# One order for VectorE's weight steps from SwiGLU on, other rooms for the last product, and outputs copied out of PSUM before they are finished

## The chip, the cores and the metric

The kernel runs on one core of one Trainium2 chip. The core has a matrix engine (TensorE, PE in the profile, with PEld for its weight loads), a vector engine (VectorE, DVE), a scalar engine (ScalarE, ACT), GpSimd (POOL), and a queue engine (SyncE, SP) that issues almost all DMA transfers. The metric is the device time of one execution in microseconds (us); lower is better.

## The reference

One layer of a decoder trunk runs on 256 tokens of width 2048, in float32. The part that the change touches is the feed-forward end of the layer:

```python
def swiglu(h, w_ffn_in, w_ffn_out):
    gate, up = jnp.split(h @ w_ffn_in, 2, axis=-1)
    return (jax.nn.silu(gate) * up) @ w_ffn_out

        h = rms_norm(x, norm2_gain[l]) * (1 + scale2) + shift2
        x = x + gate2 * swiglu(h, w_ffn_in[l], w_ffn_out[l])
```

`w_ffn_in` is 2048 x 11264 and `w_ffn_out` 5632 x 2048. Before it come conditioning (`mod`), a first norm, the input projection, three token mixers (stick-breaking attention, dilated attention, gated linear attention) and their output projection.

## The kernel before

**Arithmetic.** A float32 product is made of three matmuls on a reduced float32 format (`mm3`, lines 170 to 172): activation-high by weight-high, activation-high by weight-low, activation-low by weight-high. Each weight tile of 128 x 1024 (two 128-row chunks of 512 columns, 512 KB) is loaded once and "halved": ScalarE casts it to its high half (L166), and VectorE subtracts that from the raw tile to get the low half (L167). The halves live in `whi` and `wlo`, four rooms each, in rotation (`halves_room`).

**Rooms for raw tiles.** `raw_tile` (L149 on, issue on L159) hands out rooms in rotation: four in the `raw` pool, and then those in `rooms["extra"]`. The counter runs on over the whole kernel and is taken modulo the number of rooms. The DMA is issued on SP, which works in order: a load whose room is still in use holds up the loads behind it on that queue.

**Paired blocks.** From the second SwiGLU block on, and in the last product, two column blocks b0 and b1 are worked together for the first few row groups (`paired`, L1217 on). A group is four 128-row chunks, in two halves (`c` = 0 and 2). Its four raw tiles are r0 = (c 0, b0), r1 = (c 0, b1), r2 = (c 2, b0), r3 = (c 2, b1). From them VectorE forms four differences (`differ`, L1230): t1 = r1 - r0, t2 = r3 - t1, t3 = r3 - r1 and t4 = r2 - t2. t1 and t3 go to the first of a group's two `places`, t2 and t4 to the second. Then r0, t1, t2, r2 and t3 are halved in this order (`first`) and feed five products (`product`), six matmuls each and group. After that a loop (`rest`) takes two more row chunks of b0 (a plain halved weight) and one more halved tile (r3 of each group, then t4 of each group) per round, 18 matmuls a round. In SwiGLU there is one group (n = 1); in the last product two (n = 2). Sums of products go from a PSUM bank through `held` (ScalarE) and are added into two other banks by VectorE (L1252).

**SwiGLU.** Eleven blocks (`for i in range(NFF)`). In block i the gate columns come first and then the up columns; from i = 1 the two are paired, and the up columns go on with twelve more row chunks (L1315, six halved tiles). From the end of i = 0 the raw rooms are the pool's four and A4 and A8. The activations are h2, whose high halves lie in H0 to H3 and low halves in H4 to H7, four row chunks each; left-hand sums of h2 lie in A2 and A3. The places of the group are A13 and A14. VectorE also works on `gate2` meanwhile: steps on L287, each placed behind the last halving that had been traced (`mac`).

**The last product.** `w_fo` is `w_ffn_out`. Column blocks 0 and 1 are a pair, then 2 and 3. For n = 0 (and again n = 2) the raw rooms are the pool's four and H4 to H7; the two groups' places are A13, A14 and H2, H3. After the pair the b1 column block goes on alone over the remaining 36 row chunks. For n = 3 the last 14 row chunks are loaded as seven halved tiles, of which three have their halves in H2 to H7 (`spare`), and the two token tiles follow each other. `add_out` multiplies a PSUM bank by `gate2` (L1343), adds the residual x2 (L1345) and stores it (L1347). x2 is read back from DRAM into A2, A3, A4 and A8 (L1331).

**Order.** The framework orders the instructions of each engine by priority and by when its own model of the run has them ready, and it sets all semaphores. `prio()` raises the priority of what is inside by 4000 steps. `tc.issue_after(x)` places what it encloses behind x on x's engine and adds no semaphore.

Of the kernel before, what the change touches and what calls it, by code (L numbers as in the profile page):

```python
# [10 lines left out]
F32 = mybir.dt.float32  # L11
# [3 lines left out]
ALU = mybir.AluOpType  # L15
AX = mybir.AxisListType

P = 128
T = 256
NT = T // P  # L20
# [47 lines left out]
def trunk(ctx: ExitStack, tc: tile.TileContext, I, out):  # L68
# [16 lines left out]
    def S(tag, shape, dtype=F32):  # L85
        return slot.tile(shape, dtype, tag=tag, name=nm(tag))
# [64 lines left out]
    def raw_tile(src, ka, b, n=2):  # L151

        i = rooms["n"] % (4 + len(rooms["extra"]))
        rooms["n"] += 1
        if i < 4:
            raw = wp.tile([P, 2, NB], F32, tag="raw", name=nm("raw"))
        else:
            raw = S(rooms["extra"][i - 4], [P, 2, NB])
        nc.sync.dma_start(raw[:, :n, :], src[b][:, ka : ka + n, :])  # L159
        return raw  # L160
# [3 lines left out]

    def halve(hi, lo, raw):
        nc.scalar.copy(hi, raw)  # L166
        state["split"] = nc.vector.tensor_tensor(lo, raw, hi.bitcast(F32), op=ALU.subtract)  # L167

    def mm3(ps, lh, ll, rh, rl, start, stop, seeded=False):
        nc.tensor.matmul(ps, lh, rh, start=start, stop=False, skip_group_check=seeded)  # L170
# [1046 lines left out]
    def paired(act, sums, places, src, b0, b1, p0, p1, k1):  # L1217

        (c11, c21), (c12, c22) = p0, p1
        n = len(sums)  # L1220
        side, held = misc_bank([P, NB]), scr([P, NB])

        def halved(raw):
            hi, lo = halves_room()
            halve(hi, lo, raw)
            return hi, lo

        def differ(x, y, tag=None, into=None):
            d = S(tag, [P, 2, NB]) if into is None else into
            nc.vector.tensor_tensor(d, x, y, op=ALU.subtract)  # L1230
            return d

        with prio():
            raws = [(raw_tile(src, 4 * g, b0), raw_tile(src, 4 * g, b1)) for g in range(n)]
            raws = [r + (raw_tile(src, 4 * g + 2, b0), raw_tile(src, 4 * g + 2, b1)) for g, r in enumerate(raws)]
            first = [halved(r[0]) for r in raws]
            t1 = [differ(r[1], r[0], p[0]) for p, r in zip(places, raws)]
            first += [halved(t) for t in t1]
            t2 = [differ(r[3], t, p[1]) for p, r, t in zip(places, raws, t1)]
            first += [halved(t) for t in t2]  # L1240
            first += [halved(r[2]) for r in raws]
            first += [halved(differ(r[3], r[1], p[0])) for p, r in zip(places, raws)]
        rest = []
        for q in range(2 * n):
            g, k = q % n, 4 * n + 2 * q
            w = load_weights(src, k, k + 2, b0)
            with prio():
                rest.append((w, halved(raws[g][3] if q < n else differ(raws[g][2], t2[g], into=t2[g]))))

        def add(dst):  # L1250
            with prio(2 * AHEAD):
                nc.vector.tensor_tensor(dst, c21, held, op=ALU.add)  # L1252

        def times(ps, left, right, g, start=False):
            hi, lo = right
            for i in range(2):
                h, l = left(g, i)
                mm3(ps, h, l, hi[:, i, :], lo[:, i, :], start and i == 0, i == 1, seeded=True)

        def product(ps, left, start=False):  # L1260
            for g in range(n):
                times(ps, left, first.pop(0), g, start and g == 0)

        total = lambda q: lambda g, i: (sums[g][0][:, q, i, :], sums[g][1][:, q, i, :])
        part = lambda c, t: lambda g, i: act(4 * g + c + i, t)
        product(c11, part(0, 0), True)
        with prio(2 * AHEAD):
            nc.scalar.copy(c21, c11)
        product(side, total(0), True)
        with prio(2 * AHEAD):  # L1270
            nc.scalar.copy(held, side)
        product(c21, total(1))
        add(c12)
        product(c11, part(2, 0))
        product(c21, total(2))
        add(c22)
        for q, (w, right) in enumerate(rest):
            k = 4 * n + 2 * q
            block(p0, act, None, k, k + 2, 0, w=w, go_on=True, more=True, seeded=True)
            if q < n:  # L1280
                times(c12, total(3), right, q)
            else:
                times(c21, part(2, 1), right, q - n)
        block(p0, act, src, 8 * n, k1, b0, go_on=True, seeded=True)

    for i in range(NFF):
        pg = [acc_bank() for _ in range(NT)]
        if i == 0:
            w = load_weights(w_ff, 0, KC, 0, spare=("A12", "KD", "A9", "A10", "A0", "A1", "T1", "T2"))
            for t in range(NT):  # L1290
                block(pg, h2_at, None, 0, KC, 0, w=w, tiles=(t,))
            bg.append(gate2_bg())
            pu = [acc_bank() for _ in range(NT)]
        else:
            pu = [acc_bank() for _ in range(NT)]
            state["rate"] = (2 if i < 7 else 4) * RATE_FFN
            paired(h2_at, h2_sums, [("A13", "A14")], w_ff, i, NFF + i, pg, pu, KC)
            state["rate"] = 0.0
            if i in LATE:
                assert not macs  # L1300
                with prio():
                    act_sums.append(left_sums(LATE[i], ("A13", "A14"), *act[i - min(LATE)]))
        sgs = []
        with prio():
            for t in range(NT):
                sg = scr([P, NB])
                nc.scalar.activation(sg, pg[t], AF.Silu)
                sgs.append(sg)
        if i == 0:
            block(pu, h2_at, w_ff, 0, KC, NFF)  # L1310
            h2_sums = [left_sums(("A2", "A3"), ("A13", "A14"), h2[0][0], h2[1][0])]
            rooms["extra"] = ("A4", "A8")
        else:
            block(pu, h2_at, w_ff, 4, KC, NFF + i, go_on=True, seeded=True)
        hi = S(ftags[2 * i], [P, 4, T], F32R)  # L1315
        lo = S(ftags[2 * i + 1], [P, 4, T], F32R)
        with prio():
            for t in range(NT):
                nc.vector.tensor_mul(sgs[t], sgs[t], pu[t])

        def turn(sgs=sgs, hi=hi, lo=lo):
            for t in range(NT):
                transpose_split(sgs[t], hi, lo, t)

        later.append(turn)
        act.append((hi, lo))
    rooms["extra"] = ()
    x2 = []
    for n in range(4):
        xr = S(("A2", "A3", "A4", "A8")[n], [P, NT, NB])  # L1330
        nc.sync.dma_start(xr, x2_far[:, n])  # L1331
        x2.append(xr)

# [18 lines left out]
    K0 = 4 * len(act_sums)  # L1352
    for n in range(4):
        if n % 2 == 0:
            rooms["extra"] = ("H4", "H5", "H6", "H7")
            both = [[acc_bank() for _ in range(NT)] for _ in range(2)]
            paired(act_at, act_sums, [("A13", "A14"), ("H2", "H3")], w_fo, n, n + 1, *both, KF)
        pss = both[n % 2]
        if n == 3:
            rooms["extra"] = ()  # L1360
            block(pss, act_at, w_fo, K0, CUT, n, more=True, go_on=True, seeded=True)
            w = load_weights(w_fo, CUT, KF, n, spare=[f"H{j}" for j in range(2, 8)])
            block(pss, act_at, None, CUT, KF, 0, w=w, tiles=(0,), go_on=True, seeded=True)
            with prio():
                add_out(n, 0, pss[0])

            block(pss, act_at, None, CUT, KF - LASTK, 0, w=w, tiles=(1,), go_on=True, more=True, seeded=True)
            side = acc_bank()
            for cols, ps in ((slice(0, NB - LASTC), pss[1][:, : NB - LASTC]), (slice(NB - LASTC, NB), side[:, :LASTC])):
                for k in range(KF - LASTK, KF):  # L1370
                    wh, wl = w[k - CUT]
                    h, l = act_at(k, 1)
                    mm3(ps, h, l, wh[:, cols], wl[:, cols], k == KF - LASTK and cols.start > 0, k == KF - 1, seeded=True)
                if cols.start == 0:
                    add_out(n, 1, pss[1], end=NB - LASTC)
                    add_out(n, 1, pss[1], NB - LASTC, store=False)
            add_out(n, 1, side, NB - LASTC, base=NB - LASTC)
        else:
            if n == 1:
                block(pss, act_at, w_fo, K0, KF, n, go_on=True, seeded=True)  # L1380
            if n == 0:
                flush()
                gate2 = state["gate2"]
            with prio():
                for t in range(NT):
                    add_out(n, t, pss[t])


_INS = ["x", "c", "b_ada", "norm1_gain", "norm2_gain", "sb_q_gain", "sb_k_gain", "dil_q_gain", "dil_k_gain", "w_gla_a",
# [44 lines left out]
```

## Time and profile before

| what | value |
|---|---|
| median of three runs | 1627.28 us (1623.92, 1627.28, 1629.01) |
| the profiled execution | 1626.09 us |
| its span, first to last instruction | 1624.3 us |
| TensorE busy | 1592.4 us, 98% |
| VectorE busy | 1242.4 us, 76% |
| ScalarE busy | 855.2 us, 53% |
| DMA engines, mean busy over the span | 74% |

The page of the profile gives busy time by engine, the span in 40 slices, the chain of work that ended last, groups of instructions by line, and DMA issues. Matmuls overlap each other, so that a matmul of 0.39 us starts every 0.23 us; the start-to-start distance is what counts. Times within the run are microseconds from the start of the span. SwiGLU's second block begins near 1030 us, the last product near 1369 us, and the second pair of the last product near 1498 us.

### The profile page before, as it was taken

The numbers are of one execution on the slowest core, as the hardware profiler recorded it, in microseconds if no ns is written. First come the engines' busy times: TensorE is split into PE (matmuls) and PEld (weight loads), VectorE is DVE, ScalarE is ACT, GpSimd is POOL, SyncE is SP. The second block draws the span as 40 slices with busy tenths as digits, with TensorE's granted clock in tenths as the row PEclk, the third lists the DMA queues.
The fourth block names the chain that finished last, engine by engine and source line by source line (L and its number), as shares of the span: only waits on it lengthen the run. The fifth ranks groups of instructions, "written<-read, shape, count | busy, mean of one in ns | idle before, by whom it ended". The sixth has DMA issues, their size and how long they took to land.

```text
span 1624.3 us, 20044 instructions
## 1 busy us (share of the span) xinstructions
PE 1592.4 (98%) x7269; PEld 1311.2 (81%) x7269; DVE 1242.4 (76%) x1418; ACT 855.2 (53%) x1180; POOL 5.4 (0%) x14
## 2 busy tenths in 40 slices
PE   8999999999999999999999999999999998999999
PEld 7878888788777888888887888888888886788787
DVE  6889995877779787878657788888888875755754
ACT  5654449756587444444445555555555553534432
POOL 1000000000000000000000000000000000000000
PEclk9999999999999999999999999999999999999999
DMA  8999997874767888888776577777776666665653
GB/s 325 354 326 323 325 312 224 281 267 136 249 231 233 265 305 311 314 289 314 236 219 226 161 252 253 259 254 252 245 232 194 185 190 224 206 200 178 211 154 114
DMA packets 116179, 399.24 MB, mean 246 GB/s; under 512 B 13090, under 2 KB 13896, under 8 KB 116080
## 3 DMA queue, kind: packets, MB, share of 16 engines
q1 hardware_dynamic: 115856, 397.95, 74.0%
q8 instruction: 57, 0.93, 0.2%
q14 instruction: 42, 0.34, 0.1%
q0 software_dynamic: 224, 0.01, 0.0%
HBM read 393.71 MB, written 4.19 MB: 245 GB/s over the span
## 4 chain that ended last, share of the span: by engine, by line
PE 89%; DVE 4%; DMA 3%; ACT 2%; issue 1%; POOL 0%; DVEq 0%; ACTq 0%; POOLq 0%
PE acc L172 27%; PE acc L171 27%; PE acc L170 27%; DVE wlo L167 2%; ACT whi L166 1%; PE misc L1071 1%; DMA H<-w_ffn_out 1%; PE acc L430 1%; DMA AR<-ada_rest 1%; PE misc L786 1%; DMA raw<-w_ffn_out 1%; PE misc L170 1%; PE misc L171 1%; PE misc L172 1%; DMA raw<-w_in 0%
## 5 line engine op out<-in xcount | busy, mean ns | idle before, releaser
L166 ACT CAST whi<-raw 128x1024 fp32r<-128x1024 f32 (+1 forms) x449 | 459.4, 1028 | 483.1 <-PE acc L172 365.0
L167 DVE TENSOR_TENSOR wlo<-raw,whi 128x1024 fp32r<-128x1024 f32 (+1 forms) x449 | 531.1, 1191 | 223.0 <-ACT whi L166 219.2
L170 PE MATMUL acc<-whi,H 128*128 128x512 f32 x1476 | 578.7, 392 | 0.8 <-ACT H L442 0.4
L171 PE MATMUL acc<-wlo,H 128*128 128x512 f32 x1476 | 578.0, 392 | 1.1 <-DVE wlo L167 1.0
L172 PE MATMUL acc<-whi,H 128*128 128x512 f32 x1476 | 578.1, 392 | 1.0 <-DVE H L1157 0.6
L172 PEld LDWEIGHTS acc<-whi,H 128*128 128x128 f32 x1476 | 278.1, 189 | 59.8 <-DVE H L449 1.8
L170 PEld LDWEIGHTS acc<-whi,H 128*128 128x128 f32 x1476 | 278.1, 188 | 58.3 <-ACT H L442 1.3
L171 PEld LDWEIGHTS acc<-wlo,H 128*128 128x128 f32 x1476 | 278.1, 188 | 58.0 <-DVE wlo L167 2.2
L166 ACT CAST whi<-A 128x1024 fp32r<-128x1024 f32 x98 | 103.0, 1054 | 89.1 <-PE acc L172 85.5
L167 DVE TENSOR_TENSOR wlo<-A,whi 128x1024 fp32r<-128x1024 f32 x98 | 118.7, 1221 | 30.8 <-ACT whi L166 29.9
L170 PE MATMUL acc<-whi,A 128*128 128x512 f32 x332 | 130.5, 393 | 6.7 <-ACT whi L166 6.7
L171 PE MATMUL acc<-wlo,A 128*128 128x512 f32 x332 | 129.8, 391 | 0.0
L172 PE MATMUL acc<-whi,A 128*128 128x512 f32 x312 | 122.0, 391 | 0.0
L287 DVE SCALAR_TENSOR_TENSOR ada<-AR,csil,ada 128x1024 f32<-128x1024 f32 x59 | 75.1, 1279 | 6.8 <-DMA AR<-ada_rest 6.8
L170 PEld LDWEIGHTS acc<-whi,A 128*128 128x128 f32 x332 | 62.6, 188 | 20.6 <-ACT whi L166 7.7
L166 ACT CAST whi<-H 128x1024 fp32r<-128x1024 f32 x41 | 43.0, 1053 | 63.7 <-PE acc L172 40.4
L167 DVE TENSOR_TENSOR wlo<-H,whi 128x1024 fp32r<-128x1024 f32 x41 | 49.9, 1223 | 34.2 <-ACT whi L166 29.2
L171 PEld LDWEIGHTS acc<-wlo,A 128*128 128x128 f32 x332 | 62.6, 188 | 13.4 <-DVE wlo L167 0.4
L172 PEld LDWEIGHTS acc<-whi,A 128*128 128x128 f32 x312 | 58.8, 189 | 12.1
L170 PE MATMUL acc<-whi,T 128*128 128x512 f32 x120 | 46.8, 390 | 0.0
L172 PE MATMUL acc<-whi,T 128*128 128x512 f32 x120 | 46.7, 389 | 0.0
L171 PE MATMUL acc<-wlo,T 128*128 128x512 f32 x120 | 46.7, 389 | 0.0
(402 smaller groups left out, 1556.7 us busy)
## 6 DMA issues: line engine op xcount, KB each, us to landing
raw<-w_in SPq DMA_DIRECT2D x203, 512.0 KB, 4.9
raw<-w_ffn_in SPq DMA_DIRECT2D x122, 512.0 KB, 4.5
AR<-ada_rest SPq DMA_DIRECT2D x79, 512.0 KB, 4.8
A<-w_ffn_in SPq DMA_DIRECT2D x54, 512.0 KB, 4.4
raw<-w_ffn_out SPq DMA_DIRECT2D x53, 512.0 KB, 4.3
H<-w_ffn_out SPq DMA_DIRECT2D x35, 512.0 KB, 4.5
raw<-w_out SPq DMA_DIRECT2D x32, 512.0 KB, 4.5
KC<-ada_rest SPq DMA_DIRECT2D x30, 512.0 KB, 5.3
```

What stands on the lines that cost most here:

```text
L166: nc.scalar.copy(hi, raw)
L167: state["split"] = nc.vector.tensor_tensor(lo, raw, hi.bitcast(F32), op=ALU.subtract)
L170: nc.tensor.matmul(ps, lh, rh, start=start, stop=False, skip_group_check=seeded)
L171: nc.tensor.matmul(ps, lh, rl, start=False, stop=False, skip_group_check=seeded)
L172: state["mm"] = nc.tensor.matmul(ps, ll, rh, start=False, stop=stop, skip_group_check=seeded)
L287: nc.vector.scalar_tensor_tensor(acc, raw, c, acc, op0=ALU.mult, op1=ALU.add)
L430: state["warm"] = nc.tensor.matmul(ps, ones_r, wide, start=True, stop=True)
L786: nc.tensor.matmul(ps[:n, t * N_GLA + h, :].rearrange("p (s l) -> p s l", l=L), at(f, h, t)[:, :n], odd(at(f, h, t)), start=True, stop=True,)
L1071: nc.tensor.transpose(ps[:, i, :], src[:, i * P : (i + 1) * P], ident)
```

## The change

`halve`'s subtraction and `differ` now go through one helper, `in_order`. Once `state["ordered"]` is set, at the end of SwiGLU's first block, each of them is placed on VectorE behind the one that was traced before it. `paired` traces the differences t1 and t2 of all groups ahead of the first halving, t3 behind t1's halving, and t4 at the front of the first rounds of `rest` instead of in its last rounds. The raw tiles are loaded in the order r0, r1, r3, r2, each for all groups. In the last product the raw rooms beside the pool's four are A4 and A8 for the first pair, and A4, A8, H2 and H3 for the second; the second group's places are A2 and A3; x2 is read into H4 to H7. For n = 1 and n = 2 ScalarE first copies the two PSUM banks to a tile in H4, and `add_out` then works from there without raised priority.

```diff
     def halve(hi, lo, raw):
         nc.scalar.copy(hi, raw)
-        state["split"] = nc.vector.tensor_tensor(lo, raw, hi.bitcast(F32), op=ALU.subtract)
+        state["split"] = in_order(lo, raw, hi.bitcast(F32), op=ALU.subtract)
+
+    def in_order(*args, **kw):
+
+        with tc.issue_after(state["split"].ins) if "ordered" in state else nullcontext():
+            return nc.vector.tensor_tensor(*args, **kw)
...
         def differ(x, y, tag=None, into=None):
             d = S(tag, [P, 2, NB]) if into is None else into
-            nc.vector.tensor_tensor(d, x, y, op=ALU.subtract)
+            state["split"] = in_order(d, x, y, op=ALU.subtract)
             return d
 
         with prio():
-            raws = [(raw_tile(src, 4 * g, b0), raw_tile(src, 4 * g, b1)) for g in range(n)]
-            raws = [r + (raw_tile(src, 4 * g + 2, b0), raw_tile(src, 4 * g + 2, b1)) for g, r in enumerate(raws)]
-            first = [halved(r[0]) for r in raws]
+            raws = {(c, b, g): raw_tile(src, 4 * g + c, b) for c, b in ((0, b0), (0, b1), (2, b1), (2, b0)) for g in range(n)}
+            raws = [[raws[c, b, g] for c in (0, 2) for b in (b0, b1)] for g in range(n)]
             t1 = [differ(r[1], r[0], p[0]) for p, r in zip(places, raws)]
-            first += [halved(t) for t in t1]
             t2 = [differ(r[3], t, p[1]) for p, r, t in zip(places, raws, t1)]
-            first += [halved(t) for t in t2]
-            first += [halved(r[2]) for r in raws]
-            first += [halved(differ(r[3], r[1], p[0])) for p, r in zip(places, raws)]
+            first = [halved(r[0]) for r in raws] + [halved(t) for t in t1]
+            t3 = [differ(r[3], r[1], p[0]) for p, r in zip(places, raws)]
+            first += [halved(t) for t in t2] + [halved(r[2]) for r in raws] + [halved(t) for t in t3]
         rest = []
         for q in range(2 * n):
             g, k = q % n, 4 * n + 2 * q
+            if q < n:
+                with prio():
+                    differ(raws[g][2], t2[g], into=t2[g])
             w = load_weights(src, k, k + 2, b0)
             with prio():
-                rest.append((w, halved(raws[g][3] if q < n else differ(raws[g][2], t2[g], into=t2[g]))))
+                rest.append((w, halved(raws[g][3] if q < n else t2[g])))
...
             rooms["extra"] = ("A4", "A8")
+            state["ordered"] = True
...
-    rooms["extra"] = ()
     x2 = []
     for n in range(4):
-        xr = S(("A2", "A3", "A4", "A8")[n], [P, NT, NB])
+        xr = S(f"H{4 + n}", [P, NT, NB])
         nc.sync.dma_start(xr, x2_far[:, n])
...
         if n % 2 == 0:
-            rooms["extra"] = ("H4", "H5", "H6", "H7")
+            rooms["extra"] = ("A4", "A8", "H2", "H3")[: 2 + n]
             both = [[acc_bank() for _ in range(NT)] for _ in range(2)]
-            paired(act_at, act_sums, [("A13", "A14"), ("H2", "H3")], w_fo, n, n + 1, *both, KF)
+            paired(act_at, act_sums, [("A13", "A14"), ("A2", "A3")], w_fo, n, n + 1, *both, KF)
...
-            w = load_weights(w_fo, CUT, KF, n, spare=[f"H{j}" for j in range(2, 8)])
+            w = load_weights(w_fo, CUT, KF, n, spare=("H2", "H3", "H4", "H5", "A2", "A3"))
...
                 gate2 = state["gate2"]
+                with prio():
+                    for t in range(NT):
+                        add_out(n, t, pss[t])
+                continue
+            kept = S("H4", [P, NT, NB])
             with prio():
                 for t in range(NT):
-                    add_out(n, t, pss[t])
+                    nc.scalar.copy(kept[:, t, :], pss[t])
+            for t in range(NT):
+                add_out(n, t, kept[:, t, :])
```

## The prediction

> **What bounds the kernel now.** I read the busy time by engine in stretches of the run, then the matmuls in order of time where TensorE idles, then the chain of waits, then VectorE's and ScalarE's instructions there. In the stretch rows the columns are from:to, us, the busy us (and count) of PE, PEld, DVE, ACT and POOL, the granted TensorE clock, and the DMA engines' share.
>
> ```profile
> span 1624.3 us, 20044 instructions
> ...
> 1090.00:1133.00 43.00, 43.00 (x195) 35.68 (x194) 36.70 (x34) 22.75 (x26) 0.00 (x0) 1.00 0.77 256
> ...
> 1350.00:1369.00 19.00, 19.00 (x85) 15.73 (x84) 6.44 (x7) 6.34 (x7) 0.00 (x0) 1.00 0.68 214
> 1369.00:1400.00 31.00, 23.69 (x89) 17.86 (x88) 27.60 (x26) 16.00 (x17) 0.00 (x0) 0.89 0.50 163
> 1400.00:1498.00 98.00, 98.00 (x438) 81.22 (x437) 52.16 (x48) 40.01 (x39) 0.00 (x0) 1.00 0.66 201
> 1498.00:1520.00 22.00, 18.99 (x77) 13.86 (x76) 22.00 (x24) 12.13 (x13) 0.00 (x0) 1.00 0.50 162
> ```
>
> TensorE is the bound nearly everywhere. 1400 to 1498 holds 438 instructions in 98.00 us, eight of them transposes (0.87 us), so a matmul costs (98.00 - 0.87) / 430 = 0.226 us. A SwiGLU block has 186 matmuls and eight transposes, 42.0 + 0.9 = 42.9 us, and lasts 43.08:
>
> ```profile
> 1048.43 1.28 ACT L1307 ACTIVATE scr<-acc 128x512 f32<-128x512 f32 x2 [0.98 <-PE acc L172]
> 1091.51 1.28 ACT L1307 ACTIVATE scr<-acc 128x512 f32<-128x512 f32 x2 [0.99 <-PE acc L172]
> ```
> ```profile
> 1085.81 0.87 PE misc L1071 x8
> ```
>
> So SwiGLU has nothing to give. The loss sits at the starts of the two pairs, where TensorE idles 31.00 - 23.69 = 7.3 and 22.00 - 18.99 = 3.0 us. The matmuls there, and the last one:
>
> ```profile
> 1369.23 0.39 PE L170 MATMUL acc<-whi,A 128*128 128x512 f32 x1
> ...
> 1376.50 0.79 PE L170 MATMUL acc<-whi,A 128*128 128x512 f32 x1 [5.75 <-ACT whi L166]
> ...
> 1378.47 0.63 PE L172 MATMUL acc<-whi,A 128*128 128x512 f32 x1
> 1378.89 0.63 PE L170 MATMUL acc<-whi,A 128*128 128x512 f32 x1
> ...
> 1503.88 0.50 PE L171 MATMUL misc<-wlo,AR 128*128 128x512 f32 x1 [1.17 <-DVE wlo L167]
> ...
> 1620.08 0.28 PE L172 MATMUL acc<-H,H 128*128 128x256 f32 x1
> ```
>
> The first pair opens at E = 1369.2, stands 5.75 us, and then runs at 0.43 instead of 0.226 us a matmul. The second opens where its first twelve matmuls (2.7 us) precede the bank's copy (1501.17, below): E2 = 1498.4. From E to E2 lie 516 matmuls and eight transposes, 117.5 us; it took 129.2, a **loss of 11.7 us**. From E2 lie 504 matmuls and 24 half-width ones at 0.12, 116.8 us; it ended at 1620.2, 121.8 later: a **loss of 5.0 us**. Together 16.7 us is all that this change can win.
>
> The chain names the first wait, VectorE's and ScalarE's rows show what is behind it:
>
> ```profile
> 1370.68 4.62 DMA H<-w_ffn_out
> ```
> ```profile
> 1375.40 1.04 ACT L166 CAST whi<-H 128x1024 fp32r<-128x1024 f32 x1 [8.49 <-DMA H<-w_ffn_out]
> ```
> ```profile
> 1359.63 1.23 DVE L167 TENSOR_TENSOR wlo<-raw,whi 128x1024 fp32r<-128x1024 f32 x1 [1.50 <-ACT whi L166]
> 1366.94 1.23 DVE L167 TENSOR_TENSOR wlo<-H,whi 128x1024 fp32r<-128x1024 f32 x1 [6.08 <-ACT whi L166]
> 1368.95 1.23 DVE L1230 TENSOR_TENSOR A<-H,H 128x1024 f32<-128x1024 f32 x1 [0.79 <-DMA H<-w_ffn_out]
> ...
> 1375.33 1.23 DVE L1230 TENSOR_TENSOR H<-raw,H 128x1024 f32<-128x1024 f32 x1 [2.69 <-DMA H<-w_ffn_out]
> ```
>
> The first difference is A<-H,H and that of group 1 H<-raw,H. With r0 and r1 loaded group by group, group 1's r0 is therefore the pair's third tile in an H room; its load starts after 1369.2, so that room is H7, which the last SwiGLU matmul reads until then. VectorE ends its last SwiGLU halving at 1359.63 + 1.23 = 1360.86 and idles 6.08 us; t1 of group 1 (into H2, also read until 1369.2) starts at 1375.33.
>
> In the second pair the cause is order:
>
> ```profile
> 1477.37 1.23 DVE L1230 TENSOR_TENSOR A<-raw,raw 128x1024 f32<-128x1024 f32 x1 [1.09 <-DMA raw<-w_ffn_out]
> ...
> 1483.38 1.23 DVE L1230 TENSOR_TENSOR H<-H,raw 128x1024 f32<-128x1024 f32 x1 [1.66 <-DMA H<-w_ffn_out]
> ...
> 1490.71 1.22 DVE L1230 TENSOR_TENSOR A<-H,A 128x1024 f32<-128x1024 f32 x1 [3.55 <-DMA H<-w_ffn_out]
> 1491.85 2.35 DVE L167 TENSOR_TENSOR wlo<-raw,whi 128x1024 fp32r<-128x1024 f32 x2
> 1496.80 1.23 DVE L1230 TENSOR_TENSOR H<-raw,H 128x1024 f32<-128x1024 f32 x1 [2.59 <-DMA raw<-w_ffn_out]
> ...
> 1500.21 1.28 DVE L1343 TENSOR_TENSOR scr<-ada,acc 128x512 f32<-128x512 f32 x2
> 1501.41 1.29 DVE L1345 TENSOR_TENSOR A<-A,scr 128x512 f32<-128x512 f32 x2
> ...
> 1511.16 1.22 DVE L1230 TENSOR_TENSOR H<-raw,H 128x1024 f32<-128x1024 f32 x1
> ...
> 1513.43 1.22 DVE L1230 TENSOR_TENSOR H<-H,H 128x1024 f32<-128x1024 f32 x1
> ```
> ```profile
> 1501.17 0.57 ACT L1268 COPY acc<-acc 128x512 f32<-128x512 f32 x1 [0.30 <-PE acc L172]
> ```
>
> Differences wait 3.55 and 2.59 us for loads, with two halvings behind them that would free the rooms of such loads; then come four steps of the output (two rows of two) ahead of the pair's halvings, and VectorE is full for 22.00 of 22 us while TensorE waits. Back to back, a step of 1024 costs D = 1.135 us (two from 1511.16 to 1513.43), one of 512 costs 0.6 (two from 1500.21 to 1501.41).
>
> **The change part by part.** *First pair.* None of the six rooms is an H room now, and A2, A3 (group 1's places) fall free in SwiGLU's last pair, over 30 us ahead. The six tiles that t1 and t2 need take, in rotation, the rooms of SwiGLU's last six halvings. Late next is the sixth, r3 of group 1, whose room is freed at 1360.86; issue to landing is about 4.5 us:
>
> ```profile
> raw<-w_ffn_out SPq DMA_DIRECT2D x53, 512.0 KB, 4.3
> H<-w_ffn_out SPq DMA_DIRECT2D x35, 512.0 KB, 4.5
> ```
>
> It lands at 1365.4. The four rooms of the halves bind less: r0's is free once TensorE is three tiles short of E, 8.2 us ahead. t1, t1 and the first t2 are done by then; the second t2 takes 1365.5 to 1366.6, and r0's low half is ready at 1367.8, 1.4 us ahead of E. From 1366.6 VectorE has 12 steps of 1024 (ten halvings, two t3) and four of 512 (two L1319, two L1252): 13.6 + 2.4, so the tenth halving is ready at 1382.7. TensorE wants it after nine times six matmuls, E + 12.2 = 1381.4, plus 0.2 because the low half comes second: 1.1 late. t4 and the first weight of the rounds add 2.3 us while TensorE adds 1.4: 2.0 late. Then a round of 18 matmuls (4.1 us) faces three steps (3.4 us), and VectorE gains. The loss becomes 2.0: **-9.7 us**. No stall here is longer than those of the second pair now (1.17 us), behind which no slow matmuls stand.
>
> *Second pair.* Before and after there are eight rooms and the same load count; the rows say which falls where: t1 of group 0 is A<-raw,raw, of group 1 H<-H,raw, so that tiles one to three lie in the pool, four to seven in extra rooms, eight in the pool. Hence r1 of group 1 and r3 of group 0 come to A4 and A8, r3 of group 1 to H2, free since SwiGLU; the third tile takes at the latest the room of the last halving but one. The last halving ends 8.3 us ahead of the opening (1360.86 against E), the one before 11.0; its load lands at E2 - 6.5. Four differences end at E2 - 2.0, r0 at - 0.8. 12 steps and two L1252 make the tenth halving ready at E2 + 12.8 against 12.4, and the first weight at + 15.1 against 13.8: loss 1.3, if the output's four steps stay out, whose priority is gone: **-3.7 us**. If they fall in, 2.4 of it returns; above nothing at most the whole 5.0 goes. I take 1.3, since the halvings are raised by 4000 steps and VectorE is then never without one.
>
> *Copies.* Two for n = 1, two for n = 2, at the 0.57 us of the 1501.17 row, on ScalarE, busy 12.13 of 22 us there: hidden; if they delay casts, 1.1 us. The multiply gets no cheaper:
>
> ```profile
> L1345 DVE TENSOR_TENSOR A<-A,scr 128x512 f32<-128x512 f32 x7 | 4.6, 686 | 0.0
> L1343 DVE TENSOR_TENSOR scr<-ada,acc 128x512 f32<-128x512 f32 x7 | 4.5, 681 | 3.1 <-PE acc L172 3.1
> ```
>
> From SBUF alone 686 ns, with a PSUM operand 681. [...]
>
> *SwiGLU.* Same steps, nearly the same order: in the third block t1 and t2 (L1230) already precede r0's halving:
>
> ```profile
> 1097.56 1.23 DVE L1230 TENSOR_TENSOR A<-raw,raw 128x1024 f32<-128x1024 f32 x1 [0.33 <-DMA raw<-w_ffn_in]
> ...
> 1100.10 1.23 DVE L1230 TENSOR_TENSOR A<-A,A 128x1024 f32<-128x1024 f32 x1 [0.16 <-DMA A<-w_ffn_in]
> 1101.44 1.23 DVE L167 TENSOR_TENSOR wlo<-raw,whi 128x1024 fp32r<-128x1024 f32 x1
> ```
>
> r0 at worst moves from 1101.44 to about 1102.1, and is wanted when the up columns' last 72 matmuls end, 1091.51 + 16.3 = 1107.8. Zero; either way at most 0.5 us over ten blocks, but see the last rival.
>
> *x2 and the end.* Four loads of 512 KB move to H4 to H7 (free by 1369.2). The first use is an output step 75 us later: zero. In the last column block the spare halvings keep trace order; the last waits for its load anyway:
>
> ```profile
> 1449.00 1.28 DVE L1343 TENSOR_TENSOR scr<-ada,acc 128x512 f32<-128x512 f32 x2
> ```
> ```profile
> 1606.36 1.23 DVE L167 TENSOR_TENSOR H<-raw,H 128x1024 fp32r<-128x1024 f32 x1 [1.60 <-ACT H L166]
> ```
>
> It ends at 1607.6. The 72 full and 24 half-width matmuls of the two last passes begin at 1620.2 - 16.3 - 2.9 = 1601.0, and this tile is wanted 36 matmuls on, at 1609.2. Zero; with cover gone one step, 1.1 us.
>
> **Sum.** 16.7 - 2.0 - 1.3 gives a gain of 13.4. Each hand-over costs a few hundredths more than reckoned, over some 30 steps about 1 us (an estimate). I take 12.4: span 1611.9, execution 1626.09 - 12.4 = 1613.7. The median shown is 1.2 above this execution: **1615 us**. Bounds: nothing lost, 1610.5; the output steps, copies and last halving exposed (2.4 + 1.1 + 1.1), about 1620.
>
> **The rivals.**
>
> *A. A wait on SP takes the old one's place.* SP is in order, and the x2 loads now wait for h2's rooms, the last until 1369.2. If that load stands ahead of r3 of group 1, r3 lands at 1369.2 + 0.3 + 4.5 = 1374.0, the second t2 ends at 1375.2, r0's low half at 1376.4: a stall of 7 us, and the slow clock again, 11 matmuls by 0.2. The first pair loses about 11, the gain is 16.7 - 11 - 1.3 - 1, 1624 us. For it: the 5.75 us wait arose just so. Against: weights are raised by 4000, x2 is not. [...]
>
> *B. VectorE is the limit, not its order.* It is busy 27.60 of 31 us in the first stall. If its idle 6.08 us ahead of E are not filled because t2 starts late, only the second pair's output steps and its two DMA waits go, 3 to 4 us: 1623.5 us, about no change. Against: from 1350 to 1369 it works 6.44 of 19 us.
>
> *C. Slower: the fixed order holds SwiGLU up.* VectorE works 36.70 of 43 us there. A t2 at the front that waits for its load holds every halving and the `gate2` steps behind it, and those free rooms for loads on the same SP queue. t2 may start at 1107.8 - 2 D = 1105.5 at the latest; it starts at 1100.10 now, 5.4 us to spare. If loads come 7.5 us later than now, ten blocks lose 2 us each: 1615 + 20 = 1635 us; it is slower from 1.3 us a block on. For it: all loads share one queue, and the DMA engines are 0.77 busy (the last column but one). Against: r3 is now loaded third, not fourth.
>
> **How the numbers follow.** Forecast 0.66 (1610.5 to 1620), A 0.12, B 0.13, C 0.09. Some 0.3%, 4.9 us, is what a measurement of this kernel tells from no change, so faster means under 1622.4. The forecast all, and a third of A and B, are faster: 0.74. The rest of A and B is the same, 0.16, and C slower, with a little for the unforeseen: 0.10. The range takes the forecast's bounds and reaches over A and B: 1610 to 1624.5.
>
> **What would show it.** Right: no idle over 2 us at the pairs' openings and a clock of 1.00 there; VectorE working from 1361 to 1369; four differences, then r0, in one run; blocks of SwiGLU at 43.1 us; the output's steps behind the second pair's products. Wrong: casts that wait for a load at the first opening (A), an idle VectorE ahead of it (B), longer blocks (C).

## The result, and the profile after

The changed kernel takes 1619.57 us, median of six runs (1617.05 to 1622.37), against 1625.9 us for six runs of the kernel before (1623.92 to 1629.01). The ratio is 0.9966, with a 95% interval of 0.9951 to 0.9981: 3 to 8 us faster. Forecast were 1615 us and a gain of 12.4; the time lies inside the range of 1610 to 1624.5, and about half of the forecast gain came. Chance had a part in that: the forecast's own bounds (1610.5 to 1620) left room for the output steps, the copies and the last halving, and most of the missing time went elsewhere, into SwiGLU, as is shown below.

The profiled execution has 1617.05 us and a span of 1615.3, the lowest of the six. Set against the profiled execution of before it would show a gain of 9.0. Not all of that is the change's, as two stretch rows show, each of which runs from the start to the first silu that falls behind 1000 us (the third SwiGLU block; the columns are those of the prediction's stretch rows). First before:

```profile
0.00:1005.15 1005.15, 987.54 (x4575) 813.69 (x4576) 799.24 (x992) 554.60 (x855) 5.37 (x14) 0.99 0.80 270
```

Then after:

```profile
0.00:1002.62 1002.62, 985.83 (x4575) 811.41 (x4576) 799.48 (x992) 553.64 (x856) 5.30 (x14) 1.00 0.80 270
```

The same 4575 matmul-engine instructions took 2.5 us less, at a mean granted clock of 1.00 instead of 0.99. SwiGLU's second block begins near 935 us (not near 1030, as was said above), and the first two of the waits shown below lie in this stretch, so that the code ahead of the change took yet less (the first silu of SwiGLU's first block starts at 907.43 before and at 903.67 after). So in what follows the runs are also compared from that silu row to the last matmul, where the early part drops out.

The openings of the two pairs of the last product, in stretch rows of after:

```profile
1360.00:1372.00 12.00, 12.00 (x55) 9.93 (x53) 8.69 (x8) 4.21 (x4) 0.00 (x0) 1.00 0.77 259
1372.00:1402.00 30.00, 28.53 (x123) 22.64 (x122) 27.22 (x27) 18.46 (x19) 0.00 (x0) 1.00 0.72 245
1402.00:1492.00 90.00, 90.00 (x402) 74.60 (x402) 47.85 (x44) 36.07 (x36) 0.00 (x0) 1.00 0.65 194
1492.00:1514.00 22.00, 20.68 (x89) 16.39 (x89) 22.00 (x22) 15.09 (x17) 0.00 (x0) 1.00 0.57 190
```

TensorE idles 1.5 and 1.3 us there, where it idled 7.3 and 3.0 before, and the granted clock behind the first opening is 1.00 instead of 0.89. VectorE now works 8.69 of the 12 us ahead of the first pair. TensorE's longest waits left in the pairs, as rows of the matmuls that waited (idle time ahead and what ended it in brackets):

```profile
1379.04 0.50 PE L176 MATMUL acc<-wlo,KC 128*128 128x512 f32 x1 [1.21 <-DVE wlo L172]
...
1499.39 0.50 PE L176 MATMUL acc<-wlo,KC 128*128 128x512 f32 x1 [1.27 <-DVE wlo L172]
```

Both wait for the low half of t2. Adding up what each start-to-start distance has over 0.226 us (called the count of starts below), the pairs lose 2.3 and 1.9 us, where they lost 11.0 and 4.7 by the same count.

The other half of the account is in SwiGLU. Two successive silu rows of after are one block apart:

```profile
1046.33 1.28 ACT L1313 ACTIVATE scr<-acc 128x512 f32<-128x512 f32 x2 [0.98 <-PE acc L177]
1090.04 1.28 ACT L1313 ACTIVATE scr<-acc 128x512 f32<-128x512 f32 x2 [0.98 <-PE acc L177]
```

43.71 us, where it was 43.08. The view of waits of TensorE, over the whole of SwiGLU, from 900 to 1369 us (line, what it waited for, us, times, longest), was empty before and has one row after:

```profile
PE acc L175 <- DVE acc L1258: 3.2, 10, 0.3
```

Ten blocks, ten waits, for the addition into c12 (L1252 before). Eight of them, 2.6 us of the 3.2, lie behind 1010 us. One of them among the matmuls:

```profile
1068.57 0.39 PE L175 MATMUL acc<-whi,H 128*128 128x512 f32 x1
1069.28 0.50 PE L175 MATMUL acc<-whi,A 128*128 128x512 f32 x1 [0.33 <-DVE acc L1258]
1069.62 0.39 PE L176 MATMUL acc<-wlo,A 128*128 128x512 f32 x1
```

The idle time shown is 0.33, but the starts are 0.71 and then 0.34 apart instead of 0.226 twice, so that each wait costs 0.6 us. VectorE's rows around it, of after:

```profile
1061.74 1.23 DVE L172 TENSOR_TENSOR wlo<-A,whi 128x1024 fp32r<-128x1024 f32 x1 [0.24 <-ACT whi L166]
1062.88 1.28 DVE L1326 TENSOR_TENSOR scr<-scr,acc 128x512 f32<-128x512 f32 x2
1064.46 1.23 DVE L172 TENSOR_TENSOR wlo<-raw,whi 128x1024 fp32r<-128x1024 f32 x1 [0.29 <-ACT whi L166]
1066.26 1.22 DVE L172 TENSOR_TENSOR wlo<-A,whi 128x1024 fp32r<-128x1024 f32 x1 [0.58 <-ACT whi L166]
1067.40 1.22 DVE L172 TENSOR_TENSOR A<-raw,A 128x1024 f32<-128x1024 f32 x1
1068.54 0.69 DVE L1258 TENSOR_TENSOR acc<-acc,scr 128x512 f32<-128x512 f32 x1
```

These are t2's low half, two silu products, r2's low half, t3's low half, t4 (A<-raw,A), and the addition. The same work one block later in the run of before:

```profile
1106.93 1.23 DVE L167 TENSOR_TENSOR wlo<-A,whi 128x1024 fp32r<-128x1024 f32 x1 [0.24 <-ACT whi L166]
1108.07 1.28 DVE L1319 TENSOR_TENSOR scr<-scr,acc 128x512 f32<-128x512 f32 x2
1109.27 1.22 DVE L1230 TENSOR_TENSOR A<-raw,A 128x1024 f32<-128x1024 f32 x1
1110.40 1.22 DVE L167 TENSOR_TENSOR wlo<-raw,whi 128x1024 fp32r<-128x1024 f32 x1
1111.54 1.22 DVE L167 TENSOR_TENSOR wlo<-A,whi 128x1024 fp32r<-128x1024 f32 x1
1112.67 0.69 DVE L1252 TENSOR_TENSOR acc<-acc,scr 128x512 f32<-128x512 f32 x1
```

There t4 stood between the silu products and r2's low half, where VectorE would otherwise have waited for ScalarE's casts (0.29 and 0.58 us of such waits are in the rows of after). Now t4 stands behind t3's halving, right in front of the addition, and the casts' waits stay unused. From t2's low half to the addition it is 5.74 us before and 6.80 after.

### The profile page after: what moved, and what is told of

Same layout as the page of the kernel before. It is cut to its first block, busy times and chain, and to the rows that moved or that the text cites. A ratio compares the mean times of both kernels' runs of the same rounds, so it can differ in the third digit from the quotient of the medians.

```text
span 1615.3 us, 20044 instructions
## 1 busy us (share of the span) xinstructions
PE 1589.2 (98%) x7269; PEld 1307.1 (81%) x7269; DVE 1242.8 (77%) x1418; ACT 855.7 (53%) x1184; POOL 5.3 (0%) x14
## 4 chain that ended last, share of the span: by engine, by line
PE 84%; DVE 6%; ACT 3%; DMA 3%; issue 3%; POOL 0%; DVEq 0%; ACTq 0%; POOLq 0%
PE acc L177 26%; PE acc L176 26%; PE acc L175 26%; DVE wlo L172 3%; ACT whi L166 2%; DMA AR<-ada_rest 1%; PE misc L1076 1%; PE acc L435 1%; DVE A L172 1%; PE misc L791 1%; DMA raw<-w_ffn_out 1%; DVE acc L1258 1%; DVE ada L292 1%; PE misc L428 0%; DMA raw<-w_in 0%
## 5 line engine op out<-in xcount | busy, mean ns | idle before, releaser
L172 DVE TENSOR_TENSOR wlo<-raw,whi 128x1024 fp32r<-128x1024 f32 (+1 forms) x458 | 542.7, 1192 | 245.2 <-ACT whi L166 243.3
L166 ACT CAST whi<-raw 128x1024 fp32r<-128x1024 f32 (+1 forms) x458 | 468.5, 1027 | 490.7 <-PE acc L177 371.7
L166 ACT CAST whi<-A 128x1024 fp32r<-128x1024 f32 x124 | 130.3, 1052 | 129.4 <-PE acc L177 118.9
L172 DVE TENSOR_TENSOR wlo<-A,whi 128x1024 fp32r<-128x1024 f32 x124 | 151.0, 1223 | 58.1 <-ACT whi L166 57.7
L177 PE MATMUL acc<-whi,OS 128*128 128x512 f32 x112 | 43.6, 389 | 0.0
L491 ACT COPY A<-acc 128x512 f32<-128x512 f32 x50 | 29.0, 586 | 16.9 <-PE acc L177 15.6
```

Source lines behind the costliest of these rows:

```text
L172: return nc.vector.tensor_tensor(*args, **kw)
L177: state["mm"] = nc.tensor.matmul(ps, ll, rh, start=False, stop=stop, skip_group_check=seeded)
L491: nc.scalar.copy(A[b][:, t, :], pss[t])
```

## The experiments

Two theories of SwiGLU's loss stood against each other at the start: T1, the place of t4; T2, the new order of loads or the fixed order as such. All kernels were timed beside the kernel before. The ratio is that of all runs on record, from which the quotient of two medians differs by up to 0.0009. The last column is the time from the silu row to the last matmul in one profiled execution.

| run | median, us | ratio to before | interval | silu to last matmul, us |
|---|---|---|---|---|
| before | 1625.9 | 1 | | 614.9 |
| changed | 1619.57 | 0.9966 | 0.9951 to 0.9981 | 608.4 |
| t4 early | 1613.27 | 0.9920 | 0.9908 to 0.9932 | 603.3 |
| free in SwiGLU | 1615.29 | 0.9932 | 0.9919 to 0.9944 | 604.0 |
| rooms only | 1622.48 | 0.9968 | 0.9955 to 0.9982 | 611.3 |
| order only | 1630.51 | 1.0018 | 1.0009 to 1.0028 | 617.2 |
| no copies | 1620.69 | 0.9967 | 0.9954 to 0.9979 | 609.2 |
| extra step | 1626.78 | 0.9999 | 0.9987 to 1.0011 | 613.1 |
| output late | 1613.40 | 0.9916 | 0.9900 to 0.9932 | 602.2 |
| t3 late | 1613.31 | 0.9915 | 0.9899 to 0.9930 | 603.4 |

The first four experiments shared one chip and one set of runs of the kernel before (1627.19 us), the last four another chip and set (1625.59); across the two sets the ratios are compared.

**t4 early.** The changed kernel, with t4 back in its old place where there is one group, that is in SwiGLU.

```diff
-            first += [halved(t) for t in t2] + [halved(r[2]) for r in raws] + [halved(t) for t in t3]
+            first += [halved(t) for t in t2]
+            if n == 1:
+                differ(raws[0][2], t2[0], into=t2[0])
+            first += [halved(r[2]) for r in raws] + [halved(t) for t in t3]
...
-            if q < n:
+            if q < n and n > 1:
```

> The changed kernel, with one edit for SwiGLU's pairs only (one group): the difference t4 is traced right behind t2's halving, where the kernel before had it, instead of at the front of the rounds behind t3's halving. Theory T1: each SwiGLU block lost 0.6 us (43.71 against 43.08) because t4, one VectorE step of 1.135 us, stands between t3's halving and the first add into c12, for which TensorE then waits. T1 expects blocks of 43.1 us, no matmul that waits for that add, about 6 us less than the changed kernel: 1613.5 us, ratio 0.993 to before, the last product as in the changed kernel. Rival T2: the blocks are longer because r3 is loaded ahead of r2, or because the fixed order makes VectorE wait for casts, whatever the place of t4. T2 expects blocks of 43.5 us or more and 1617 to 1620 us.

VectorE's rows of this run:

```profile
1064.68 1.22 DVE L172 TENSOR_TENSOR A<-raw,A 128x1024 f32<-128x1024 f32 x1
1065.82 1.22 DVE L172 TENSOR_TENSOR wlo<-raw,whi 128x1024 fp32r<-128x1024 f32 x1
1066.95 1.22 DVE L172 TENSOR_TENSOR wlo<-A,whi 128x1024 fp32r<-128x1024 f32 x1
1068.08 0.70 DVE L1261 TENSOR_TENSOR acc<-acc,scr 128x512 f32<-128x512 f32 x1
```

t4, r2's low half, t3's low half and the addition follow one another without a gap. The view of waits shows none for TensorE in SwiGLU, the next four blocks take 43.32, 43.09, 43.10 and 43.07 us (the first of them holds other work too, and took 43.28 before), and the whole is 6 us under the changed kernel, with intervals that do not meet (5.1 us from the silu row on, behind which eight of the ten blocks lie). T2 falls: the loads and the fixed order are still those of the change.

**Free in SwiGLU.** The fixed order begins only behind SwiGLU's last block.

```diff
             rooms["extra"] = ("A4", "A8")
-            state["ordered"] = True
...
+    state["ordered"] = True
     x2 = []
```

> The changed kernel, with the fixed order switched on only behind SwiGLU's last block; the order of tracing and of loads is that of the changed kernel in SwiGLU too. T1 expects that without the fixed order t4 falls back into a gap ahead of t3's halving: blocks of 43.1 us, 1613.5 us, ratio 0.993. T2 in the form of the load order expects 43.7 us blocks as before this edit, 1619.5 us; T2 in the form of waits made by the fixed order expects 43.1 too, so that e1 and not this run tells it from T1.

Blocks of 43.1 us and 1615.3 us. The load order, which is the changed one here too, costs nothing. Left free, t4 moves forward by itself; the intervals of this run and the one above overlap, so that the fixed order brings SwiGLU no gain that these runs show.

**Rooms only.** The kernel before, with the room lines of the diff alone (A4, A8, H2, H3 for raw tiles, A2 and A3 as places, x2 in H4 to H7, the spare list).

> The kernel before with the other rooms only (A4 and A8, then also H2 and H3, for raw tiles; A2 and A3 as places; x2 in H4 to H7), no fixed order, the old tracing and the outputs straight from PSUM. My account gives the first pair's loss (11.7 us before, 2.3 in the changed kernel) to the rooms: the first stall of 5.75 us and the slow clock behind it are gone, the first pair loses 2 to 4 us, the second pair still about 5, SwiGLU blocks stay at 43.08: 1617 us, ratio 0.9945. The rival, that the order of the differences did it, expects that most of the first pair's loss stays: 1623 us or more.

The 5.75 us stall is gone, as expected, but the gain is only about 5 us by the ratio, and 3.6 from the silu row on. The matmuls of this run show another stall, at the rounds of the first pair, and slow ones behind it:

```profile
1376.51 0.50 PE L171 MATMUL acc<-wlo,KC 128*128 128x512 f32 x1 [0.39 <-DVE wlo L167]
...
1396.75 1.22 PE L170 MATMUL acc<-whi,A 128*128 128x512 f32 x2 [3.14 <-ACT whi L166]
...
1399.03 0.63 PE L171 MATMUL acc<-wlo,A 128*128 128x512 f32 x1
1399.46 0.63 PE L172 MATMUL acc<-whi,A 128*128 128x512 f32 x1
...
1509.48 0.49 PE L170 MATMUL acc<-whi,AR 128*128 128x512 f32 x1 [0.83 <-ACT whi L166]
1510.43 0.50 PE L170 MATMUL acc<-whi,A 128*128 128x512 f32 x1 [0.45 <-ACT whi L166]
1511.38 0.51 PE L170 MATMUL acc<-whi,KC 128*128 128x512 f32 x1 [0.45 <-ACT whi L166]
...
1513.51 0.63 PE L171 MATMUL acc<-wlo,A 128*128 128x512 f32 x1
1513.94 0.63 PE L172 MATMUL acc<-whi,A 128*128 128x512 f32 x1
```

ScalarE's row says what the 3.14 us are spent on, and a row of VectorE and one of the DMA queue say what held that load:

```profile
1388.91 1.22 DVE L1230 TENSOR_TENSOR A<-A,A 128x1024 f32<-128x1024 f32 x1
...
1390.16 0.33 SPq L159 DMA_DIRECT2D A<-w_ffn_out  x1
...
1395.66 1.99 ACT L166 CAST whi<-A 128x1024 fp32r<-128x1024 f32 x2 [8.88 <-DMA A<-w_ffn_out]
```

With six rooms and the old order of loads the third round's weight takes the room of r2 of group 0. The last step that reads that r2 is t4 (A<-A,A), which the old order puts into the last two rounds: it ends at 1390.13, and the load goes out at 1390.16. The first pair loses about 8 us by the count of starts (11.0 before), the second 4.3, nearly as before. So rooms alone take away the first wait and make a smaller one; my figure of 2 to 4 us for this run was too low.

**Order only.** The changed kernel with the old rooms, old places, old x2 rooms, and outputs straight from PSUM.

> The changed kernel with the rooms, places and x2 rooms of before and the outputs straight from PSUM: the fixed order and its tracing alone. My account: in the first pair every halving stands behind t1 of group 1, whose operand still waits for H7, so TensorE stands about 9 to 10 us and then runs at the slow rate, a loss of 12 to 15; the second pair loses 3 to 4; SwiGLU loses 6: about 1632 us, ratio 1.004, slower than before. The rival, that the order brings the gain whatever the rooms, expects 1620 us or less.

1630.51 us, slower than before. The first pair's opening:

```profile
1382.83 0.80 PE L175 MATMUL misc<-whi,KC 128*128 128x512 f32 x1 [5.88 <-ACT whi L166]
...
1386.21 0.80 PE L176 MATMUL acc<-wlo,A 128*128 128x512 f32 x1 [2.59 <-DVE wlo L172]
```

All halvings stand behind a difference whose operand waits for H7 (it is t1 of group 0, not of group 1 as expected), so TensorE stands 5.88 and 2.59 us and runs slow afterwards (0.80 us for the matmul in both rows, 0.39 in a full stream), a loss of 11.7 us by the count of starts; SwiGLU has its 43.7 us blocks; the second pair loses 1.4 us by the count, where 3 to 4 were expected. So it is the order that helps the second pair, even with its outputs raised as before.

**No copies.** The changed kernel with `add_out` straight from PSUM, raised, for all n.

> The changed kernel without the copies: n = 1 and n = 2 finish straight from PSUM, raised, as before. In the changed kernel three of the four output steps of n = 1 fell between the second pair's halvings anyway (1.8 us ahead of t2's halving). My account: the fourth step joins them, and c12's bank comes free later, so the second pair loses 2.5 to 3.5 us instead of 1.9; the whole 1620.2 us, that is within 1 us or so of the changed kernel, ratio about 0.997. The rival, that the copies carry much of the second pair's gain, expects a loss near the 5.0 us of before: 1622.5 us, ratio 0.9985.

1620.69 us, ratio 0.9967 against 0.9966. The second pair loses 2.9 us instead of 1.9 in the profile, which the times can't tell apart. By the profile the copies bring 0.7 us from the silu row on; the intervals of the two ratios would allow some 3 us either way.

**Extra step.** The changed kernel with the suspected cost doubled.

```diff
                 with prio():
+                    if n == 1:
+                        state["split"] = in_order(t2[g], t2[g], t2[g], op=ALU.max)
                     differ(raws[g][2], t2[g], into=t2[g])
```

> The changed kernel with one more VectorE step of 1024 (the maximum of t2 with itself, which leaves t2 as it is) just ahead of t4 in SwiGLU's pairs only: the dose of the suspected cost doubled. T1 (the step stands ahead of the add for which TensorE waits) expects each of the ten blocks longer by the whole step, 1.13 us: 43.7 to 44.85, 11 us in all, about 1631 us, ratio 1.0035. The rival, that VectorE has room there and the 0.6 us came from elsewhere, expects blocks of 43.7 to 43.9 and under 1622 us.

Blocks of 44.36 us and 1626.78 us: neither theory's number. T1 had the sign, and expected 44.85. VectorE's rows (L1260 is the addition here) and the matmuls:

```profile
1073.91 1.22 DVE L172 TENSOR_TENSOR A<-A 128x1024 f32<-128x1024 f32 x1
1075.05 0.69 DVE L1260 TENSOR_TENSOR acc<-acc,scr 128x512 f32<-128x512 f32 x1
1075.65 1.21 DVE L172 TENSOR_TENSOR A<-raw,A 128x1024 f32<-128x1024 f32 x1
```
```profile
1075.80 0.50 PE L175 MATMUL acc<-whi,A 128*128 128x512 f32 x1 [0.32 <-DVE acc L1260]
...
1078.05 0.50 PE L176 MATMUL acc<-wlo,H 128*128 128x512 f32 x1 [0.37 <-DVE wlo L172]
```

The scheduler put the addition between the extra step (A<-A) and t4. So again one step stands ahead of the addition, for the same 0.48 us at that matmul, and t4 behind it delays the low half of the first round's weight, for another 0.54. A step in that place costs about 0.6 us, twice in the same block in eight of the ten blocks (the second wait is shorter in the last two), whichever step it is: VectorE has some 0.5 us to spare there and no more (an estimate, 1.135 less 0.6).

**Output late, and t3 late.** t4 early, with the output steps of n = 1 put behind the last halving of the second pair's rounds (through `issue_after`, traced after that pair; those of n = 2 are then traced one column block later, too). Then the same with t3 traced behind t2's halvings in the last product.

> The version with t4 early (first experiment) and the output steps of n = 1 placed behind the last halving of the second pair's rounds. The second pair's stall is 1.56 us ahead of t2's halving there, with three output steps (1.8 us) in front of it. My account: they go, the stall falls to 0.2 or less, the second pair loses 0.5 instead of 1.9: 1611.9 us, ratio 0.991. The rival, that the two t3 differences in front of t2's halving are enough by themselves, expects the stall to stay above 1 us and no change against the first experiment, 0.992.

> The same with t3 traced behind t2's halvings instead of ahead of them, in the last product's pairs only. My account: in the first pair the stall of 1.04 us ahead of t2's halving goes; VectorE's work up to the rounds stays the same, so part comes back later, at t3's halving and at the first weight of the rounds: the first pair loses 1.3 to 2 instead of 2.3, the second 0.5 or less: 1611.3 us, ratio 0.9905. The rival, that only the total of VectorE's work counts, expects the same loss as without this move, 1611.9 us.

In the first of the two the second pair's stall ahead of t2's low half falls from 1.39 us of idle time to 0.38:

```profile
1495.77 0.50 PE L176 MATMUL acc<-wlo,KC 128*128 128x512 f32 x1 [0.38 <-DVE wlo L172]
```

The place is confirmed, and the size is somewhat under what was expected: the second pair loses 1.0 us by the count instead of 2.0, where 0.5 was expected, and from the silu row to the last matmul it is 1.1 us less. The times, 0.9916 against 0.9920, can't tell it. Moving t3 as well takes the first pair's stall away from t2's halving and puts 1.45 us at r2's. Its profile is 1.2 us longer than without this move, but there r3 of group 1 also landed later: the second t2 starts 2.5 us ahead of the opening, where it was 3.6. The medians are the same (1613.31 and 1613.40). So the gain of 0.6 us that I expected does not show, and the rival, by which only the total of VectorE's work up to the rounds counts, fits the times; these runs do not prove it. All three versions with t4 early beat both kernels; which of them is fastest is open.

## Why the prediction was right, and where it was not

- **TensorE is the bound, and 16.7 us at the two pairs can be won**: held. The changed kernel lost 4.2 us there by the count of starts, 15.7 before: a gain of 11.5 in the pairs, where the forecast had 12.4 once its 1 us for the hand-overs was taken off. No run shows that 1 us by itself; in before the matmul that waited 5.75 us started 0.06 us behind the end of the cast it waited for (1376.50 against 1375.40 + 1.04).
- **First pair, loss 2.0**: 2.3. r3 of group 1 was loaded when the last SwiGLU halving freed its room, as reckoned, and took 5.2 us instead of 4.5 (issued 1363.42, t2 starts 1368.62), which the 1.4 us of reserve covered. The stall lay ahead of t2's low half and not at the rounds, since the two t3 stand in front of t2's halvings; the sum was nearly right, its place was not.
- **Second pair, loss 1.3**: 1.9. The step that failed is "VectorE is then never without one": two multiplies and one addition of the output (1.8 us) fell between the halvings. The last experiments show both the place and that it is worth about 1 us.
- **Copies at nothing**: held, and they bring nothing that the times can tell: the run without them has the same ratio (0.9967 against 0.9966). In the profile of after the multiply takes 691 ns a step from the copy in SBUF (four steps of 512) and 683 with an operand in PSUM (three).
- **SwiGLU at zero, "at most 0.5 us over ten blocks"**: this is the step that failed, 0.6 us in each of ten blocks, 6 us in all and half of the gain. I followed r0's halving, at the front of a block, and found 5 us of room. I did not follow t4, which the change moves from behind t2's halving to behind t3's, ahead of the addition for which TensorE waits. The row that would have said it was there: the addition of before begins right behind t3's low half (1111.54, 1112.67), with no gap in between.
- **x2 and the end at zero**: held. Of the four loads of x2 two went out ahead of r3 of group 1 and two behind it. None held it: r3's load went out at 1363.42, as the halving that frees its room ended (1363.39, VectorE's row of 1362.17 and its 1.22 us):

```profile
1343.86 0.33 SPq L1337 DMA_DIRECT2D H<-x_far  x1
...
1361.13 0.38 SPq L1337 DMA_DIRECT2D H<-x_far  x1
...
1363.42 0.33 SPq L159 DMA_DIRECT2D raw<-w_ffn_out  x1
...
1366.93 0.33 SPq L1337 DMA_DIRECT2D H<-x_far  x1
...
1373.04 0.38 SPq L1337 DMA_DIRECT2D H<-x_far  x1
```

- **Rivals**: A fell by these rows of the DMA queue (in before the queue did stand so: no load went out between the one of 1363.98 and 1370.25, and then two within 0.81 us), and B by VectorE's 8.69 busy us ahead of the first pair. C had the sign and the place (the fixed order holds SwiGLU up), but another mechanism: no t2 waited for a load; a step of 1.135 us took a place in which 0.5 us was free. It had to cost 1.3 us a block to make the kernel slower, and cost 0.6.
- **The time**: by the count of starts the pairs gain 15.7 - 4.2 = 11.5. From the silu row on, eight blocks lose 0.63 each, 5.0, which leaves 6.5; the two profiled executions differ by 6.5 there (614.9 and 608.4). With all ten blocks it is 5.2, against 6.3 between the medians, whose interval of 3 to 8 us holds it.

## What to carry to other kernels

When a fixed order is laid on an engine that is busy 85% of a stage, follow every step that it moves to the next instruction that another engine waits for, not only the first one; a step is free only in a gap that it can still reach. In the pairs rooms alone won 3.6 us and the order alone 2.8, and both together 11.5, because a front of differences needs its operands loaded, and early loads need an order that frees their rooms. Compare two profiles from a common row behind the code that did not change: here SwiGLU's first silu, ahead of which no version was changed, starts anywhere from 903.67 to 908.55 us in the ten profiled executions.

## What the hardware showed that was not expected

The slow matmuls (0.43 us from start to start) did not need one long wait in these runs. In the run with the rooms only, three idle times of 0.83, 0.45 and 0.45 us within 3 us, with only the matmul that had waited between one and the next, were followed by seven slow matmuls from 1512.66 on. The run of before has the same three waits (0.86, 0.46 and 0.44 us, up to 1515.48), and from 1516.17 on the matmuls behind them are 0.23 to 0.24 apart. The length of one wait does not tell the cases apart: behind the 1.17 us ahead of 1503.88 in before the matmuls are 0.23 to 0.34 apart. The granted clock tells the two runs apart. Stretch rows of the run with the rooms only:

```profile
1508.96:1512.37 3.41, 1.99 (x6) 1.11 (x7) 3.41 (x4) 3.32 (x4) 0.00 (x0) 1.00 0.82 252
1512.37:1515.78 3.41, 3.41 (x10) 2.64 (x9) 3.41 (x5) 1.04 (x1) 0.00 (x0) 0.50 0.98 348
```

And of before, around the first two of its waits:

```profile
1511.35:1514.76 3.41, 2.09 (x7) 1.17 (x7) 3.41 (x4) 2.27 (x3) 0.00 (x0) 1.00 0.39 94
```

In the clock record of before, the three stretches at half the clock that begin and end inside the run are 3.41, 6.83 and 6.83 us long; they begin at 473.70, 886.71 and 1374.82, which is 121 and 143 times 3.413 us apart. In after there is one, at 884.61, 3.41 us long. So in these two traces the changes of the clock fall on the edges of windows of 3.41 us, and the stretches of the rows above are windows of that length; the second row of the run with the rooms only has 0.50 over one of them. At 0.226 us a matmul, the window ahead of the slow matmuls holds 1.20 us of matmul work, a share of 0.35. In before the third wait falls into the next window, and the window shown holds 1.52 us, a share of 0.45. Counted in this way over the traces of before and after (an estimate: matmuls weighed by their columns, the first and last 10 us left out, windows at the full clock alone), the windows with shares of 0.00, 0.20 and 0.32 in before and of 0.20 in after were followed by half the clock; one of 0.30 in after, and all those of 0.44 and more in both, were not.

The wait of TensorE at 1069.28 in after cost nearly twice the idle time that the profile puts to it (0.33 us idle, 0.60 in the starts). The profile counts the idle time from the end of the matmul ahead, 0.39 us after its start, where in a full stream the next one would have started after 0.226; and the matmul behind the one that waited started 0.34 us after it.
